# A hybrid decoder block on one core: 48 instead of 40 dense expert columns, gate2 through DRAM, and buffers laid out anew

## The chip, the cores and the metric

The kernel runs on one core of one Trainium2 chip. The metric is the device time of one execution in microseconds. The kernel before took 2249.88 us, the median of three runs (2248.31 to 2253.04).

## What is computed

One layer works on 256 tokens of width 2048 (D), in float32. A condition vector goes through one matrix, `w_ada`, and gives six vectors of length D, of which the last, gate2, scales the second sub-layer. The first sub-layer mixes tokens (gated linear recurrences and a state-space scan). The second, which the change is about, is a mixture of 16384 experts with one neuron each:

```python
# reference, cut
mod = silu(c) @ w_ada + b_ada                       # shift1, scale1, gate1, shift2, scale2, gate2
x  = x + gate1 * mix(norm(x))
h2 = rms_norm(x, norm2_g) * (1 + scale2) + shift2
# 8 heads; each takes its 16 best of 128 x 128 experts by two lists of 128 keys
expert, gate = topk_softmax(h2 @ w_q, sub_keys)     # 256 tokens x 128 experts
act = gelu(einsum(h2, u_tab[expert]))               # u_tab, v_tab: 16384 x 2048 float32
out = rms_norm(x + gate2 * einsum(gate * act, v_tab[expert]), final_norm_g)
```

`u_tab` and `v_tab` are 134 MB each. Counted from the reference's inputs, the 256 tokens choose 32768 experts; written as 128 columns of 128 experts (an expert's column is its index modulo 128), 23,659 of the choices lie in columns 0 to 87 and 21,400 in columns 0 to 79.

## The kernel before

The program is written out by hand, and each engine runs its instructions in the written order. Weights arrive in tiles `raw` of 128x1024 (512 KB), four of them at a time, loaded by SyncE's queue (and every second one by ScalarE's queue for the last part). ScalarE rounds each to a high part, VectorE subtracts for the low part (`issue_split`, lines 138 and 147), and TensorE multiplies high and low parts (`hl`, four buffers).

After the first sub-layer and the query projection come three stretches that concern us.

**The U stretch** (`u_quad`, line 1262). All activations of the first J1 = 88 columns are computed, four columns at a time: 22 quads of 8 steps, each step one `raw` tile of `u_t` and 12 matmuls of 512 columns. A quad's 128x2x512 result is stored to a DRAM table `ad`. Beside it runs background work with a budget (`bg_pay`, 1.0 a step): the top-16 searches on VectorE, then 32 one-hot steps (`onehot`, `g_step`) that scatter the gates of the last JD = 40 columns into a dense table `Wt`, and the gate2 section of `w_ada`: from step 26 on, one load of 128x256 a step (128 loads, four buffers, three loads ahead) and one multiply-add on VectorE (`gate2_tick`). Before the last quad but one, four steps (`g2_steps`) turn gate2 into two 128x1024 tiles with TensorE and ScalarE; before the last quad everything in the background is flushed, the buffers of that time are released, and two tiles of 128x4x2048 (`vs`) are cleared and first filled.

**The dense columns.** For each of the JD last columns, `u_slot` multiplies h2 with the column of `u_t` (two tiles, 16 matmuls of 512 and 16 of 256 columns), applies GELU and multiplies into `Wt`. Then, for each half of the output width, `v_slot` multiplies `Wt` with the column of `v_t` (one tile, 12 matmuls of 512) into four PSUM banks.

**The sparse experts** run beside the dense columns. A group of four tokens is one of 64 sparse quads: four GpSimd gathers fetch the up to 128 rows of `v_t` (8 KB each) of one token, rows of dense columns being skipped by a bounds check; four more fetch the 128 activations from `ad` (`w_gather`); `v_quad` (line 1343) multiplies the rows with the weights `Wz` in 16 matmuls of 32x512. There are buffers for two quads, so the gathers of quad q+2 wait until `v_quad(q)` has read its tiles. `tick` is called twice in each `u_slot` and once after each `v_slot`, 4*JD = 160 times, and issues a sparse quad whenever

```python
if n >= 6 and sq["n"] < 62 * (n - 3) // (4 * JD - 4):
    sparse()
```

that is after two or three ticks in turn (62 quads over 157 ticks). The last two quads follow the last tick.

`rows_load` fetches, at three places among the `v_slot`s, the two halves of x (from DRAM, 1 MB each) and the final norm's gain repeated on 128 partitions (1 MB) into the tile `H` that held h2. `merge` multiplies a PSUM bank with gate2 into a part of `H`, adds it to x, and squares the sum on ScalarE; `final` normalises and stores.

Of the kernel before, what the change touches and what calls it, by code (L numbers as in the profile page):

```python
# [19 lines left out]
D = 2048  # L20
# [3 lines left out]
JD = 40  # L24
# [9 lines left out]
NQ = 4  # L34
ETILES = [72]
# [22 lines left out]
def hybrid_kernel(ctx, tc, xT, cols, w_ada, w_in, lru_w, w_o1, w_o2, w_q, keys, u_t, v_t, fng, out):  # L58
# [11 lines left out]
    def bank(n):  # L70
        return psum.tile([128, 512], FT, name=f"b{n}")

# [566 lines left out]
    def lru_gates(b, i):  # L639
        h = 4 * b + i  # L640
        xc = LR["xc"][:, i]
        Z = {}

        def g_pe():
            w = LR["w"].pop(h)
            Z["p"] = p = bank(4 - (i + GD) % 2)
            for s in range(2):
                pe.matmul(p[:, s * 256:(s + 1) * 256], w[:, s], xc, start=True, stop=True)
            lru_w_load()

        def g_ew():
            if i == 0:
                LR.update(a=keep.tile([128, 4, 256], FT, name="X0"),
                          m=keep.tile([128, 4, 256], FT, name="X1"),
                          gx=keep.tile([128, 4, 256], FT, name="X2"))
# [60 lines left out]
    def evac(e, ps):  # L716
# [8 lines left out]
        elif e >= 48:  # L725
            after = None
            if e >= 64:
                g = e % 4
                if e < 68:
                    S["BC"] = S["BCs"][:, g % 2]  # L730
                    for n, t in enumerate(("xs", "zs")):
                        S[t] = (mix.tile([128, 4, 256], FT, name=t) if g == 3 else
                                keep.tile([128, 4, 256], FT, name=f"X{2 * (g % 2) + n}"))
# [77 lines left out]
    def x_load(i):  # L811
        x2[i] = keep.tile([128, 4, 256], FT, name=f"X{i}")
        sp.dma_start(x2[i], xT[:, 4 * i:4 * i + 4, :])
# [178 lines left out]
    g2 = [keep.tile([128, 1024], FT, name=f"X{i}") for i in range(2)]  # L992
# [151 lines left out]
    def g2_steps(q):  # L1144
        P = {}

        def g_pe():
            P[0] = b = gbank()
            for i in range(4):
                k = 4 * q + i  # L1150
                pe.matmul(b[:, i * 128:(i + 1) * 128], bc(mod[:, 5, k:k + 1], 128, 128), ident,
                          start=True, stop=True)

        def g_ew():
            act.activation(g2[q // 2][:, (q % 2) * 512:(q % 2 + 1) * 512], P[0], AF.Copy)
# [12 lines left out]
    def gate2_tick():  # L1168
        n = gt["n"]
        if n >= 128:  # L1170
            return
        q, k = divmod(n, 16)
        if n == 0:
            for _ in range(3):
                gate2_load()
        gate2_load()
        w = gt.pop(n)
        if k == 0:
            gt["a"] = s1.tile([128, 256], FT, name="adga", bufs=2)
# [4 lines left out]
        if k == 15:  # L1184
            a = gt["a"]

            def fin():
                p = gbank()
                for i in range(2):
                    pe.matmul(p[:, i:i + 1], a[:, i * 128:(i + 1) * 128], ones[:, 0:1], start=True, stop=True)  # L1190
                defer(lambda: dve.tensor_add(mod[:, 5, 2 * q:2 * q + 2], p[:, :2], col("b_ada", 80 + 2 * q, 2)))
# [29 lines left out]
    NG = 8  # L1221

    def onehot():
# [5 lines left out]
        a = s1.tile([128, NG, 128], F8, name="oha", bufs=4)  # L1229
        o = s1.tile([128, NG, 2, JD], F16, name="ohb", bufs=4)  # L1230
# [29 lines left out]
    ad = dram.tile([T, E1], FT, name="ad")  # L1260

    def u_quad(n, pay):
        ps = [bank(2 * (n % 2) + tb) for tb in range(2)]
        for kp in range(8):
# [14 lines left out]
            if it >= 26:  # L1279
                gt["slot"] = it  # L1280
                gate2_tick()
# [53 lines left out]
    def v_quad(q):  # L1335
# [4 lines left out]
        for c in range(4):  # L1340
            for g in range(4):
                x = 32 + 32 * (4 * (q % NW) + g) - m
                pe.matmul(sb[c][32 * g:32 * g + 32, :], Wz[:, x:x + 32], vs[q % 2][:, g, c * 512:(c + 1) * 512],  # L1343
# [92 lines left out]
    nm = [0]  # L1436
# [9 lines left out]
    def merge(tb, c, ps):  # L1446
        s = slice(c * 512, (c + 1) * 512)
        nm[0] += 1
        t = R["t"][:, 3, (nm[0] % 4) * 512:(nm[0] % 4 + 1) * 512]
        dve.tensor_tensor(t, ps, g2[c // 2][:, (c % 2) * 512:(c % 2 + 1) * 512], op=OP.mult)  # L1450
        a = R["t"][:, tb, s]
        dve.tensor_tensor(a, a, t, op=OP.add)
# [22 lines left out]
    for n in range(NU):  # L1475
        if n == 1:
            gbk[:] = [6, 7, 4, 5]
        if n == NU - 2:
            bg.extend(g2_steps(q) for q in range(4))
        if n == NU - 1:  # L1480
            bg_flush()
            assert gt["n"] == 128 and not pedue and len(gpend) == 0
            s1s.close()
            qp = ctx.enter_context(tc.tile_pool(name="qp", bufs=1))
            for i in range(2):
# [93 lines left out]
```

## Time and profile before

| | before |
|---|---|
| median of the timed runs | 2249.88 us |
| profiled execution | 2229.45 us |
| its span, first to last instruction | 2227.7 us |
| TensorE matmul busy | 2073.1 us, 93% of the span |
| VectorE / ScalarE / GpSimd busy | 65% / 38% / 42% |
| moved by DMA | 626.38 MB |
| granted TensorE clock, mean | 0.971 |

The profile is one execution, taken with the hardware profiler; a line number such as L1343 is a line of the kernel, and "PE b L1343 <- DMA vq" means that TensorE stood idle before an instruction of that line until a transfer into `vq` had landed. A matmul's end is modelled, so matmuls overlap in the rows, and the step from one start to the next is the better measure of what one costs. `PEld` is TensorE's loading of weights, beside the matmuls.

### The profile page before, as it was taken

How to read it: one execution, taken by the hardware profiler on the slowest of the kernel's cores; microseconds unless marked ns; L12 is line 12 of the kernel's file. 1: busy time of each engine (PE TensorE's matmuls, PEld its weight loads, DVE VectorE, ACT ScalarE, POOL GpSimd, SP SyncE). 2: the span in 40 equal slices, each digit the busy share in tenths (PEclk: the TensorE clock that was granted, in tenths of full speed). 3: DMA queues.
4: the chain of work that ended last, by engine and by line, in shares of the span. 5: the costliest groups of instructions: out<-in, count | busy, mean ns of one | idle time of the engine just before them, and what ended most of it. 6: DMA issues, size and time to landing. Idle time of an engine off the chain costs nothing.

```text
span 2227.7 us, 34204 instructions
## 1 busy us (share of the span) xinstructions
PE 2073.1 (93%) x12675; PEld 1619.3 (73%) x12675; DVE 1437.3 (65%) x2135; ACT 929.0 (42%) x1421; POOL 855.4 (38%) x730
## 2 busy tenths in 40 slices
PE   4889999999999999999999999999999999989996
PEld 3888999978999888888788888755555555445553
DVE  6987887988878868779989974433233343324333
ACT  2335565666644454444345444322222232223232
POOL 0002333222112010001224424377777776667774
PEclk6889999999999999999999999999999999999998
DMA  9956666667789854677777778699999999998996
GB/s 350 383 193 203 216 202 219 224 222 258 265 300 324 323 171 161 199 237 244 253 243 244 245 247 293 209 366 355 340 341 348 357 356 344 362 365 327 353 363 242
DMA packets 261686, 626.38 MB, mean 281 GB/s; under 512 B 36261, under 2 KB 144933, under 8 KB 237093
## 3 DMA queue, kind: packets, MB, share of 16 engines
q1 hardware_dynamic: 204672, 387.72, 51.4%
q0 software_dynamic: 45056, 194.01, 23.1%
q10 hardware_dynamic: 11792, 42.47, 5.5%
q8 instruction: 99, 1.62, 0.3%
q14 instruction: 67, 0.55, 0.1%
HBM read 682.97 MB, written 15.73 MB: 314 GB/s over the span
## 4 chain that ended last, share of the span: by engine, by line
PE 52%; DMA 23%; DVE 11%; issue 8%; ACT 2%; POOL 2%; POOLq 0%; SPq 0%; DVEq 0%; ACTq 0%
DMA vq<-in_v_t,X 19%; PE b L426 7%; PE b L1271 6%; PE b L1273 6%; PE b L1272 6%; PE b L1343 4%; PE b L428 3%; PE b L1426 3%; DVE hl L147 3%; PE b L898 3%; DVE aa L247 2%; PE b L792 2%; PE b L794 2%; PE b L793 2%; PE b L899 1%
## 5 line engine op out<-in xcount | busy, mean ns | idle before, releaser
L138 ACT ACTIVATE hl<-raw 128x1024 fp32r<-128x1024 f32 x578 | 612.1, 1061 | 1155.6 <-PE b L428 356.5
L147 DVE TENSOR_TENSOR hl<-raw,hl 128x1024 fp32r<-128x1024 f32 x578 | 745.8, 1295 | 138.7 <-ACT hl L138 137.5
L426 PE MATMUL b<-H,hl 128*128 128x512 f32 x1248 | 447.5, 402 | 3.1 <-DVE qT L432 2.8
L1311 POOL DMA_INDIRECT vq<-in_v_t,X x256 | 301.6, 1178 | 139.8 <-DMA vq<-in_v_t,X 60.9
L428 PE MATMUL b<-H,hl 128*128 128x256 f32 x1248 | 349.9, 280 | 5.2 <-DVE hl L147 5.2
L1343 PE MATMUL b<-vq,Wz 128*32 128x512 f32 x2048 | 290.5, 625 | 57.1 <-DMA vq<-in_v_t,X 49.7
L1321 POOL DMA_INDIRECT X<-ad,X x256 | 273.1, 1067 | 124.1 <-issue 72.9
L426 PEld LDWEIGHTS b<-H,hl 128*128 128x128 f32 x1248 | 234.4, 188 | 84.8 <-issue 25.7
L1271 PE MATMUL b<-hl,H 128*128 128x512 f32 x704 | 278.6, 396 | 0.0
L1273 PE MATMUL b<-hl,H 128*128 128x512 f32 x704 | 274.8, 390 | 3.0 <-DVE hl L147 2.9
L1272 PE MATMUL b<-hl,H 128*128 128x512 f32 x704 | 274.5, 390 | 0.0
L1343 PEld LDWEIGHTS b<-vq,Wz 128*32 128x32 f32 x2048 | 69.0, 113 | 240.9 <-issue 143.0
L428 PEld LDWEIGHTS b<-H,hl 128*128 128x128 f32 x1248 | 235.5, 189 | 6.8 <-DVE hl L147 6.6
L1426 PE MATMUL b<-hl,X 128*128 128x512 f32 x960 | 230.2, 396 | 4.7 <-ACT X L419 3.2
L1426 PEld LDWEIGHTS b<-hl,X 128*128 128x128 f32 x960 | 177.9, 189 | 70.1 <-issue 26.9
L1333 DVE TENSOR_TENSOR Wz<-X 128x4 f32<-128x4 f32 x64 | 10.5, 166 | 286.9 <-ACT X L1329 215.4
L794 PE MATMUL b<-H,hl 128*128 128x256 f32 x560 | 159.2, 284 | 6.2 <-DVE hl L147 6.2
L792 PE MATMUL b<-H,hl 128*128 128x256 f32 x560 | 161.4, 288 | 0.0
L793 PE MATMUL b<-H,hl 128*128 128x256 f32 x560 | 158.7, 283 | 0.0
L1273 PEld LDWEIGHTS b<-hl,H 128*128 128x128 f32 x704 | 132.6, 188 | 32.2 <-DVE hl L147 4.2
L1272 PEld LDWEIGHTS b<-hl,H 128*128 128x128 f32 x704 | 132.7, 189 | 25.9
L1271 PEld LDWEIGHTS b<-hl,H 128*128 128x128 f32 x704 | 132.5, 188 | 25.9
(312 smaller groups left out, 3083.6 us busy)
## 6 DMA issues: line engine op xcount, KB each, us to landing
raw<-in_u_t SPq DMA_DIRECT2D x216, 512.0 KB, 4.3
raw<-in_w_in SPq DMA_DIRECT2D x146, 512.0 KB, 4.8
adr<-in_w_ada SPq DMA_DIRECT2D x96, 512.0 KB, 4.9
adw<-in_w_ada SPq DMA_DIRECT2D x64, 512.0 KB, 8.4
raw<-in_w_o SPq DMA_DIRECT2D x64, 512.0 KB, 5.4
raw<-in_u_t ACTq DMA_DIRECT2D x40, 512.0 KB, 7.6
raw<-in_v_t SPq DMA_DIRECT2D x40, 512.0 KB, 8.3
raw<-in_v_t ACTq DMA_DIRECT2D x40, 512.0 KB, 8.0
```

The costliest lines, as they stand in the source:

```text
L138: act.activation(t[:, 0], r, AF.Copy)
L147: dve.tensor_sub(t[:, 1], r, t[:, 0].bitcast(FT))
L426: pe.matmul(ps, w[:, 0, c], x[:, k].rearrange("p a b -> p (a b)"), start=(k == 0), stop=False, skip_group_check=True)
L428: pe.matmul(ps[:, :256], w[:, 1, c], x[:, k, 0], start=False, stop=(k == 15), skip_group_check=True)
L792: pe.matmul(ps, wh, hT[:, k, 0, :], start=(k == 0), stop=False)
L1271: pe.matmul(o, hh, w[:, 0, :, kk], start=(k == 0), stop=False)
L1272: pe.matmul(o, hl_, w[:, 0, :, kk], start=False, stop=False)
L1273: pe.matmul(o, hh, w[:, 1, :, kk], start=False, stop=(k == 15))
L1311: pool.indirect_dma_start(x, None, vf, bass.IndirectOffsetOnAxis(ap=eV[:, t:t + 1], axis=0), bounds_check=E1 - 1, oob_is_err=False)
L1321: pool.indirect_dma_start(wA[:, 4 * q + g:4 * q + g + 1], None, adf, bass.IndirectOffsetOnAxis(ap=eW[:, t:t + 1], axis=0), bounds_check=T ...
L1343: pe.matmul(sb[c][32 * g:32 * g + 32, :], Wz[:, x:x + 32], vs[q % 2][:, g, c * 512:(c + 1) * 512], start=(m == 0), stop=(m == 31), skip_gr ...
L1426: pe.matmul(ob[tb * 2 + c], w[:, i, s], v[:, k, c * 512:(c + 1) * 512], start=(jj == 0 and (i, k) == (0, 0)), stop=(jj == JD - 1 and k == 1))
```

## The change

JD goes from 40 to 48: J1 falls from 88 to 80 columns, so that there are 20 U quads, 48 `u_slot`s, 96 `v_slot`s and 192 ticks; the 64 sparse quads skip the rows of 48 columns instead of 40. The wider dense table needs room, and that is what the rest does:

- the tiles X0 and X1 become halves of one tile X01; in the U stretch its halves hold the four buffers of the first one-hot operand and two (instead of four) buffers of the gate2 loads; the second one-hot operand has three buffers instead of four;
- the gate2 section of `w_ada` comes in 64 loads of 128x512, one at every second step from step 22, one load ahead; its sums are closed four times instead of eight;
- the four `g2_steps` go. gate2 is stored from its 128x16 tile to DRAM (`g2d`) before the last U quad and read back, repeated on 128 partitions, into the fourth part of `H` at the first `rows_load`;
- `merge` multiplies the PSUM bank in place, adds from PSUM, and lets the square go to PSUM;
- the gather buffers are eight tiles of 128x2048 instead of two of 128x4x2048, the last of them in X01.

```diff
-JD = 40
+JD = 48
@@
+NG = 8
@@
+    pair = keep.tile([128, 8, 256], FT, name="X01")
+
+    def xbuf(i):
+        return pair[:, 4 * i:4 * i + 4] if i < 2 else keep.tile([128, 4, 256], FT, name=f"X{i}")
@@
-    g2 = [keep.tile([128, 1024], FT, name=f"X{i}") for i in range(2)]
+    two = keep.tile([128, 8, 256], FT, name="two", tag="X01")
+    ohs = two[:, :4].rearrange("p a b -> p (a b)").bitcast(F8).rearrange("p (n t i) -> p n t i", n=4, t=NG)
+    ads = two[:, 4:]
@@
-    def g2_steps(q):
...
-        return g_pe, g_ew, 0.3
@@ def gate2_load():
-        if n < 128:
+        if n < 64:
             q, k = divmod(n, 16)
-            gt[n] = s1.tile([128, 256], FT, name="adg", bufs=4)
-            sp.dma_start(gt[n], w_ada[k * 128:(k + 1) * 128, 5 * D + q * 256:5 * D + (q + 1) * 256])
+            gt[n] = ads[:, 2 * (n % 2):2 * (n % 2) + 2].rearrange("p a b -> p (a b)")
+            sp.dma_start(gt[n], w_ada[k * 128:(k + 1) * 128, 5 * D + q * 512:5 * D + (q + 1) * 512])
@@ def gate2_tick():
         if n == 0:
-            for _ in range(3):
-                gate2_load()
+            gate2_load()
         gate2_load()
@@ def onehot():
-        a = s1.tile([128, NG, 128], F8, name="oha", bufs=4)
-        o = s1.tile([128, NG, 2, JD], F16, name="ohb", bufs=4)
+        a = ohs[:, n % 4]
+        o = s1.tile([128, NG, 2, JD], F16, name="ohb", bufs=3)
@@ def u_quad(n, pay):
-            if it >= 26:
+            if it >= 22 and it % 2 == 0:
@@ def v_gather(q):
-            x, t = vs[q % 2][:, g], tok(q, g)
+            x, t = vs[4 * (q % 2) + g], tok(q, g)
@@ def rows_load(n):
             R["t"] = keep.tile([128, 4, D], FT, name="H")
+            sp.dma_start(R["t"][:, 3], bass.AP(tensor=g2d.tensor, offset=g2d.offset, ap=[[0, 128], [1, D]]))
@@ def merge(tb, c, ps):
-        t = R["t"][:, 3, (nm[0] % 4) * 512:(nm[0] % 4 + 1) * 512]
-        dve.tensor_tensor(t, ps, g2[c // 2][:, (c % 2) * 512:(c % 2 + 1) * 512], op=OP.mult)
+        dve.tensor_tensor(ps, ps, R["t"][:, 3, s], op=OP.mult)
         a = R["t"][:, tb, s]
-        dve.tensor_tensor(a, a, t, op=OP.add)
+        dve.tensor_tensor(a, a, ps, op=OP.add)
@@
-            act.activation(t, a, AF.Square, accum_out=rf[:, tb, c:c + 1])
+            act.activation(ps, a, AF.Square, accum_out=rf[:, tb, c:c + 1])
@@ for n in range(NU):
-        if n == NU - 2:
-            bg.extend(g2_steps(q) for q in range(4))
         if n == NU - 1:
@@
-            for i in range(2):
-                vs[i] = qp.tile([128, 4, D], FT, name=f"vq{i}")
+            sp.dma_start(g2d.rearrange("o (k p) -> p (o k)", p=128), mod[:, 5])
+            for i in range(8):
+                vs[i] = (qp.tile([128, D], FT, name=f"vq{i}") if i < 7 else
+                         keep.tile([128, D], FT, name="vq7", tag="X01"))
                 pool.memset(vs[i], 0.0)
-                v_gather(i)
+                if i % 4 == 3:
+                    v_gather(i // 4)
```

Line numbers shift by a few: L1333 becomes L1327, L147 becomes L153, L130 becomes L136, L1166 becomes L1160.

Where instructions stand now is seen at three places. The first is VectorE's order in the dense columns. `Wz` is the write of the weights for one sparse quad, so it marks the quads; each `hl` row is the low part of one `raw` tile, of which there is one a tick. Before, from one quad over two more:

```order
L1333 TENSOR_TENSOR Wz<-X_7824 128x4
L147 TENSOR_TENSOR hl<-raw,hl 128x1024
L1397 TENSOR_TENSOR Wt<-Wt,xt 128x256
L432 TENSOR_TENSOR xt<-b_14544,xt 128x256
L147 TENSOR_TENSOR hl<-raw,hl 128x1024 x2
L1397 TENSOR_TENSOR Wt<-Wt,xt 128x256
L432 TENSOR_TENSOR xt<-b_14633,xt 128x256
L1333 TENSOR_TENSOR Wz<-X_7824 128x4
L147 TENSOR_TENSOR hl<-raw,hl 128x1024 x2
L1397 TENSOR_TENSOR Wt<-Wt,xt 128x256
L432 TENSOR_TENSOR xt<-b_14720,xt 128x256
L1333 TENSOR_TENSOR Wz<-X_7824 128x4
```

And of the change, from one quad to the next and on to the row ahead of a third:

```order
L1327 TENSOR_TENSOR Wz<-X_7811 128x4
L153 TENSOR_TENSOR hl<-raw,hl 128x1024 x2
L1391 TENSOR_TENSOR Wt<-Wt,xt 128x256
L438 TENSOR_TENSOR xt<-b_14928,xt 128x256
L153 TENSOR_TENSOR hl<-raw,hl 128x1024
L1327 TENSOR_TENSOR Wz<-X_7811 128x4
L153 TENSOR_TENSOR hl<-raw,hl 128x1024
L1391 TENSOR_TENSOR Wt<-Wt,xt 128x256
L438 TENSOR_TENSOR xt<-b_14977,xt 128x256
L153 TENSOR_TENSOR hl<-raw,hl 128x1024 x2
L1391 TENSOR_TENSOR Wt<-Wt,xt 128x256
L438 TENSOR_TENSOR xt<-b_15066,xt 128x256
```

Before, three tiles and then two lie between quads; now three and three (62 quads over 189 ticks).

The second place is SyncE's queue where the gate2 section begins, in the U stretch. `raw` is a weight tile, `adg` a gate2 load, `ad` the store of a quad's result. Before:

```order
L130 DMA raw<-in_u_t 128x4x256
L1166 DMA adg<-in_w_ada 128x256 x4
L130 DMA raw<-in_u_t 128x4x256
L1166 DMA adg<-in_w_ada 128x256
L130 DMA raw<-in_u_t 128x4x256
L1166 DMA adg<-in_w_ada 128x256
```

Of the change, where `two` is the tile in X01 whose second half holds the gate2 loads:

```order
L1160 DMA two<-in_w_ada 128x512 x2
L136 DMA raw<-in_u_t 128x4x256 x2
L1160 DMA two<-in_w_ada 128x512
L136 DMA raw<-in_u_t 128x4x256
L1283 DMA ad<-X_9271 128x2x512
L136 DMA raw<-in_u_t 128x4x256
L1160 DMA two<-in_w_ada 128x512
```

A load of twice the size now stands behind every second weight tile, with one load ahead instead of three.

The third place is the same queue at the end of the U stretch and at the start of the `v_slot`s. Before:

```order
L1289 DMA ad<-X_13215 128x2x512
L130 DMA raw<-in_u_t 128x4x256
L130 DMA raw<-in_u_t 128x1024 x40
L130 DMA raw<-in_v_t 128x1024 x4
L1442 DMA H<-x2d 128x2048
```

Of the change:

```order
L1283 DMA ad<-X_12594 128x2x512
L1475 DMA g2d<-mod 128x16x1
L136 DMA raw<-in_u_t 128x4x256
L136 DMA raw<-in_u_t 128x1024 x48
L136 DMA raw<-in_v_t 128x1024 x4
L1434 DMA H<-g2d 128x2048
L1436 DMA H<-x2d 128x2048
```

The store of gate2 is now ahead of the last U tile, and the repeated read of it ahead of the first half of x.

More of the change, by code (lines that the diff above doesn't have):

```diff
@@ L652, in g_ew @@
             if i == 0:
-                LR.update(a=keep.tile([128, 4, 256], FT, name="X0"),
-                          m=keep.tile([128, 4, 256], FT, name="X1"),
+                LR.update(a=xbuf(0),
+                          m=xbuf(1),
                           gx=keep.tile([128, 4, 256], FT, name="X2"))
@@ L732, in evac @@
                         S[t] = (mix.tile([128, 4, 256], FT, name=t) if g == 3 else
-                                keep.tile([128, 4, 256], FT, name=f"X{2 * (g % 2) + n}"))
+                                xbuf(2 * (g % 2) + n))
                 o = S["BC"][:, (e - 64) // 4]
@@ L811, in x_load @@
     def x_load(i):
-        x2[i] = keep.tile([128, 4, 256], FT, name=f"X{i}")
+        x2[i] = xbuf(i)
         sp.dma_start(x2[i], xT[:, 4 * i:4 * i + 4, :])
@@ L1142, in q_evac @@
             bg.extend(g_step(n) for n in range(32))
-    def g2_steps(q):
[L1145 to L1155, printed above, removed]
-        return g_pe, g_ew, 0.3
     gt = {"n": 0, "ld": 0}
@@ L1162, in gate2_load @@
         gt["ld"] += 1
-        if n < 128:
+        if n < 64:
             q, k = divmod(n, 16)
-            gt[n] = s1.tile([128, 256], FT, name="adg", bufs=4)
-            sp.dma_start(gt[n], w_ada[k * 128:(k + 1) * 128, 5 * D + q * 256:5 * D + (q + 1) * 256])
+            gt[n] = ads[:, 2 * (n % 2):2 * (n % 2) + 2].rearrange("p a b -> p (a b)")
+            sp.dma_start(gt[n], w_ada[k * 128:(k + 1) * 128, 5 * D + q * 512:5 * D + (q + 1) * 512])
     def gate2_tick():
         n = gt["n"]
-        if n >= 128:
+        if n >= 64:
             return
@@ L1178, in gate2_tick @@
         if k == 0:
-            gt["a"] = s1.tile([128, 256], FT, name="adga", bufs=2)
+            gt["a"] = (pr.tile([128, 512], FT, name="adgx", tag="xt") if q % 2 else
+                       s1.tile([128, 512], FT, name="adga"))
             dve.tensor_scalar(gt["a"], w, cact[:, 0:1], None, op0=OP.mult)
@@ L1188, in fin @@
                 p = gbank()
-                for i in range(2):
+                for i in range(4):
                     pe.matmul(p[:, i:i + 1], a[:, i * 128:(i + 1) * 128], ones[:, 0:1], start=True, stop=True)
-                defer(lambda: dve.tensor_add(mod[:, 5, 2 * q:2 * q + 2], p[:, :2], col("b_ada", 80 + 2 * q, 2)))
+                defer(lambda: dve.tensor_add(mod[:, 5, 4 * q:4 * q + 4], p[:, :4], col("b_ada", 80 + 4 * q, 4)))
             pedue.append((gt["slot"] + 2, fin))
@@ L1260, in hybrid_kernel @@
     ad = dram.tile([T, E1], FT, name="ad")
+    g2d = dram.tile([1, D], FT, name="g2d")
     def u_quad(n, pay):
@@ L1342, in v_quad @@
                 x = 32 + 32 * (4 * (q % NW) + g) - m
-                pe.matmul(sb[c][32 * g:32 * g + 32, :], Wz[:, x:x + 32], vs[q % 2][:, g, c * 512:(c + 1) * 512],
+                pe.matmul(sb[c][32 * g:32 * g + 32, :], Wz[:, x:x + 32], vs[4 * (q % 2) + g][:, c * 512:(c + 1) * 512],
                           start=(m == 0), stop=(m == 31), skip_group_check=True)
@@ L1477, in hybrid_kernel @@
             gbk[:] = [6, 7, 4, 5]
-        if n == NU - 2:
-            bg.extend(g2_steps(q) for q in range(4))
         if n == NU - 1:
             bg_flush()
-            assert gt["n"] == 128 and not pedue and len(gpend) == 0
+            assert gt["n"] == 64 and not pedue and len(gpend) == 0
             s1s.close()
             qp = ctx.enter_context(tc.tile_pool(name="qp", bufs=1))
-            for i in range(2):
-                vs[i] = qp.tile([128, 4, D], FT, name=f"vq{i}")
+            sp.dma_start(g2d.rearrange("o (k p) -> p (o k)", p=128), mod[:, 5])
+            for i in range(8):
+                vs[i] = (qp.tile([128, D], FT, name=f"vq{i}") if i < 7 else
+                         keep.tile([128, D], FT, name="vq7", tag="X01"))
                 pool.memset(vs[i], 0.0)
-                v_gather(i)
+                if i % 4 == 3:
+                    v_gather(i // 4)
         u_quad(n, 1.0)
```

3 lines of the change are left out of this document (removed).

## The prediction, made blind

> **What bounds the kernel now.** I read the page first, then busy time by stretch, then who waits for whom in the stretches that change, then single rows in order of time.
>
> ```profile
> PE 2073.1 (93%) x12675; PEld 1619.3 (73%) x12675; DVE 1437.3 (65%) x2135; ACT 929.0 (42%) x1421; POOL 855.4 (38%) x730
> ...
> DMA  9956666667789854677777778699999999998996
> GB/s 350 383 193 203 216 202 219 224 222 258 265 300 324 323 171 161 199 237 244 253 243 244 245 247 293 209 366 355 340 341 348 357 356 344 362 365 327 353 363 242
> ```
>
> TensorE is busy nearly everywhere, but from slice 27 on DMA is at nine tenths too: the last 800 us have two limits close together. The view of busy time by stretch separates the U stretch (first row), the `u_slot`s (second), the `v_slot`s (third) and the end:
>
> ```profile
> core 0: us, PE busy (x) PEld busy (x) DVE busy (x) ACT busy (x) POOL busy (x), PEclk, DMA share, GB/s
> 895.00:1409.00 514.00, 509.63 (x2726) 418.86 (x2725) 423.09 (x652) 234.77 (x304) 127.32 (x86) 1.00 0.76 246
> 1409.00:1804.00 395.00, 364.64 (x2241) 227.76 (x2239) 127.81 (x191) 114.48 (x197) 284.76 (x246) 0.99 0.91 336
> 1804.00:2200.00 396.00, 370.02 (x1984) 211.85 (x1984) 138.93 (x208) 109.68 (x192) 278.44 (x256) 0.97 0.93 348
> 2200.00:2228.00 28.00, 10.76 (x64) 2.56 (x64) 14.71 (x28) 8.51 (x19) 2.98 (x3) 0.77 0.51 188
> ```
>
> In U, TensorE is idle for 4.4 of 514 us: it alone sets the pace there. In the next 791 us it waits for the gathers; these are the PE rows of the waits, U first and the dense columns second:
>
> ```profile
> PE b L1273 <- DVE hl L147: 2.9, 2, 2.6
> ```
>
> ```profile
> PE b L1343 <- DMA vq<-in_v_t,X: 48.1, 35, 3.2
> ```
>
> The ends of matmuls are modelled, so part of the waiting hides in long bursts, and starts tell more. TensorE's rows in order of time, where a burst of L1343 is one sparse quad (x32) and a tick is 12 matmuls of L1426:
>
> ```profile
> 1429.41 3.09 PE L1343 MATMUL b<-vq,Wz 128*32 128x512 f32 x16 [3.27 <-issue]
> ...
> 1569.00 3.64 PE L1343 MATMUL b<-vq,Wz 128*32 128x512 f32 x32
> 1578.42 1.25 PE L1343 MATMUL b<-vq,Wz 128*32 128x512 f32 x6
> ...
> 1883.67 3.64 PE L1343 MATMUL b<-vq,Wz 128*32 128x512 f32 x32
> 1887.24 5.73 PE L1426 MATMUL b<-hl,X 128*128 128x512 f32 x24
> 1892.91 1.06 PE L1343 MATMUL b<-vq,Wz 128*32 128x512 f32 x6
> 1895.72 3.62 PE L1343 MATMUL b<-vq,Wz 128*32 128x512 f32 x26 [1.75 <-DMA vq<-in_v_t,X]
> 1899.27 8.49 PE L1426 MATMUL b<-hl,X 128*128 128x512 f32 x36
> 1907.69 1.06 PE L1343 MATMUL b<-vq,Wz 128*32 128x512 f32 x6
> ...
> 2193.26 3.64 PE L1343 MATMUL b<-vq,Wz 128*32 128x512 f32 x32
> ```
>
> A quad without a wait takes 3.57 us (1883.67 to 1887.24). Three v ticks take 8.42 (1899.27 to 1907.69), 2.81 each; two u ticks 5.85 (1578.42 less 1569.00 less 3.57), 2.92 each. The quad at 1892.91, after two ticks, takes 6.36, so it waits 2.79. Measured in this way over the 62 quads from the first row to the last, what exceeds 3.57 us sums to 102.3 us, and it falls almost wholly on one kind: 29 quads behind two ticks wait 90.3 us (3.1 each), 32 behind three ticks 10.3 us (0.32 each), the first 1.7.
>
> **The change part by part.** I sum against the profiled execution's 2229.45 us (span 2227.7 and 1.75 around it). It lies 20.4 us under the median of 2249.88; I carry the difference over to the median unchanged.
>
> *Two U quads fewer.* ScalarE's evacuations mark the ends of quads:
>
> ```profile
> 1322.24 1.13 ACT L1286 ACTIVATE X<-b 128x512 f32<-128x512 f32 x2
> 1343.47 1.07 ACT L1286 ACTIVATE X<-b 128x512 f32<-128x512 f32 x2
> 1365.68 1.07 ACT L1286 ACTIVATE X<-b 128x512 f32<-128x512 f32 x2
> 1390.25 1.07 ACT L1286 ACTIVATE X<-b 128x512 f32<-128x512 f32 x2
> ```
>
> By the order of the program the one-hot steps end with the 18th quad in both, so what goes are quads with nothing beside them: 1322.24 to 1365.68, **-43.4**. The quad with the `g2_steps` took 24.57 against their mean of 21.72: **-3** (their matmuls, L1151 below, are 4.2 us busy).
>
> *Wider one-hot steps, other gate2 loads.*
>
> ```profile
> L1247 PE MATMUL b<-ohb,oha 128*128 128x40 f16 x512 | 18.5, 180 | 1.0 <-POOL ohb L1236 0.7 <-POOL ohb L1235 0.3
> ...
> L1151 PE MATMUL b<-ident,mod 128*128 128x128 f32 x32 | 4.2, 274 | 0.0
> ```
>
> 512 matmuls of 40 columns become 48 wide: nothing if something other than columns sets their time, a fifth of 18.5 = 3.7 if columns do; I take the middle, **+2**. The one-hot work on VectorE and GpSimd grows by a fifth too, behind a TensorE that lacked 2.9 us of VectorE's in all of U.
>
> ```profile
> L1182 DVE SCALAR_TENSOR_TENSOR adga<-adg,cact,adga 128x256 f32<-128x256 f32 x120 | 72.8, 607 | 0.6 <-DMA adg<-in_w_ada 0.6
> ```
>
> ```profile
> L247 DVE SCALAR_TENSOR_TENSOR aa<-adw,cact,aa 128x512 f32<-128x512 f32 x112 | 76.8, 748 | 0.6 <-DMA adw<-in_w_ada 0.6
> ```
>
> On VectorE 120 of 607 ns become 60 of 748: 28 us less, worth nothing where VectorE isn't waited for. The loads have less lead: a step is 21.72/8 = 2.7 us, so two steps (5.4 us) instead of three (8.1).
>
> ```profile
> DMA to landing us min/median/max: 3.3/4.5/7.3
> ```
>
> ```profile
> raw<-in_u_t SPq DMA_DIRECT2D x216, 512.0 KB, 4.3
> ...
> X<-ad,X POOLq DMA_INDIRECT x256, 2.3
> ...
> H<-x2d SPq DMA_DIRECT2D x2, 1024.0 KB, 9.1
> ...
> H<-in_fng SPq DMA_DIRECT2D x1, 1024.0 KB, 13.8
> ```
>
> The first row is that of the gate2 loads of 128 KB; the 512 KB tiles land in 4.3. So 256 KB at about 4.5 fits into 5.4 and the slowest (7.3) is 1.9 late. Behind a late multiply-add on VectorE stand the `hl` subtractions, for which TensorE waits once its four `hl` buffers are used up. Bounds: 0, and 64 x 1.9 = 122 with every load the slowest and no cover; I take **0**, by the median.
>
> *The store of gate2*: 2048 pieces of 4 bytes. Nearest is the gather of 128 pieces of 4 bytes, 2.3 us: between 2.3 and 16 x 2.3 = 37 us. Behind it in SyncE's queue stands one U tile, then the `u_slot`s' tiles; four loaded and four split tiles are ahead of TensorE, some 8 x 2.7 = 22 us of cover, so 0 to 15; I take **+2**, near the gather. The Trainium skill (DMA: Bandwidth & Descriptors, Rules for kernel authors) speaks against this store: a last dimension that isn't contiguous is cut into one descriptor per element and should be rearranged. With the 10.5 ns a packet of its Bandwidth section the store would take an estimated 21.5 us, which would add up to 20 to my sum if nothing hid it; no row before shows it.
>
> *The dense columns.* Without any waiting, TensorE needs before 80 x 2.92 + 80 x 2.81 + 62 x 3.57 = 679.7 us; 791 less this and less 102.3 of waits leaves 9 for the rest. Of the change: 96 x 2.92 + 96 x 2.81 + 62 x 3.57 = 771.4. What of the waits stays? All quads now stand behind three ticks, the kind that waited 0.32 us: 62 x 0.32 = 19.8. Bytes allow it: 395 us at 336 and 396 at 348 GB/s are 270.5 MB; 2259 rows of 8 KB fewer are gathered (-18.5 MB), 32 tiles of 512 KB come (+16.8), and 1.05 MB of gate2, so 269.8. GpSimd issues as many gathers as before, and the granted clock was 0.97 to 0.99 here. The repeated read of gate2 is 1.05 MB at 342 GB/s, 3 us, if it moves like the rest; the repeated read of the gain took 13.8 us to land against 9.1 for as many bytes of x, so up to 5 more; I take **3**. A bank now comes free after the add, not after the multiply:
>
> ```profile
> L1452 DVE TENSOR_TENSOR H<-H 128x512 f32<-128x512 f32 x4 | 2.8, 692 | 0.1
> L1450 DVE TENSOR_TENSOR H<-b,X 128x512 f32<-128x512 f32 x4 | 2.7, 686 | 6.6 <-PE b L1343 6.6
> ```
>
> Reading PSUM (L1450) costs no more than SBUF (L1452); an add of 0.7 us for each of four banks is 0 to 2.8 where the halves change, **+1**. Writing PSUM isn't shown; the two rows being alike, I price it as SBUF, 0 with under 1 us either way. Sum: 771.4 + 19.8 + 9 + 3 + 1 = 804.2 against 791: **+13**. The 28 us of the end have the same two quads and stores.
>
> Together: -43.4 - 3 + 2 + 2 + 13 = **-29**, to 2200 in the profiled execution and **2220** as a median.
>
> **The rivals.**
>
> *DMA has room, and no quad waits.* The share of 0.91 to 0.93 isn't full, and slice 2 moved 383 GB/s. Against it: even three-tick quads waited 0.32. The dense columns then take 771.4 + 9 + 1 = 781, -10; total -52, **2198**. The Trainium skill (HBM Reference, Specifications) sides with this rival: a core that streams alone can reach about 425 GB/s, well above what I saw here.
>
> *The waits come back in part.* Three-tick quads waited little because the two-tick quad before each had waited and let the gathers run ahead; now nothing does. At 0.7 us each: 771.4 + 43.4 + 13 = 828, +37, total -6, **2244**.
>
> *The gathers keep their latency: slower.* If a quad waits as long on average whatever the distance (102.3/62 = 1.65 us), the 92 us of new matmuls are paid in full: 771.4 + 102.3 + 13 = 887, +96, total +53, **2303**. It decides from 0.79 us a quad, where the 42 us gained in U are used up. Against it: 0.32 behind three ticks, and equal bytes.
>
> *Late gate2 loads*: if a quarter are 1.9 us late and nothing hides it, 16 x 1.9 = 30: total +1, **2251**. Against it: the median of 4.5.
>
> *The store of gate2 stalls the queue*: 15 instead of 2, total -16, **2234**.
>
> **How the numbers follow.** Forecast 0.54 (its own range 2206 to 2232), room on DMA 0.16, waits in part 0.13, slower 0.08, late loads 0.05, store 0.04. The range reaches from 2190, under the second, to 2246, over the third, and leaves out the slow rival and most of the late loads. A measurement can tell 0.2%, 4.5 us. Faster: 0.54 + 0.16 + 0.08 of the third + 0.04 = 0.82; within: 0.03 + 0.04 = 0.07; slower: 0.02 + 0.08 + 0.01 = 0.11.
>
> **What would show it.** The U stretch should be 467 to 474 us, its last evacuations 21 to 23 us apart, with a few us of waits for `hl`; more waits, or waits of L1182's successor for its loads, mean late loads. The 62 quads should start about 12.2 us apart and exceed 3.57 us by 20 us in sum: under 5 means the first rival, over 49 the slow one. Rows of `raw` behind the store should land as before. The forecast is wrong if the dense columns take under 785 or over 820 us.

## The result, and the profile after

| | before | change |
|---|---|---|
| median of the timed runs | 2249.64 us (4 runs, 2248.31 to 2253.04) | 2214.41 us (4 runs, 2210.67 to 2220.39) |
| profiled execution | 2229.45 us | 2215.8 us |
| span | 2227.7 us | 2213.8 us |

The ratio of the runs is 0.9844 [0.9818, 0.9869]: 35.2 us by the medians, where 29 were forecast. The two profiled executions are only 13.7 us apart, and this difference between the medians and the profiles is the first thing to explain. Here and below, medians and ratios leave out runs that took over 1.5% longer than the fastest of their kernel.

Busy time by stretch of the change: the U stretch, the `u_slot`s, the `v_slot`s, the end (columns as in the prediction: engines' busy time, granted clock, DMA share, GB/s):

```profile
895.00:1370.00 475.00, 465.42 (x2504) 381.02 (x2503) 399.84 (x568) 217.19 (x280) 153.25 (x92) 0.99 0.74 244
1370.00:1770.00 400.00, 391.29 (x2489) 266.92 (x2489) 150.31 (x217) 133.11 (x221) 288.88 (x245) 0.99 0.90 328
1770.00:2185.00 415.00, 395.82 (x2186) 250.01 (x2184) 165.01 (x242) 134.18 (x230) 278.69 (x256) 0.98 0.92 337
2185.00:2213.80 28.80, 10.38 (x64) 2.96 (x64) 16.41 (x30) 8.69 (x19) 3.97 (x4) 0.77 0.48 176
```

U takes 475 us instead of 514, the dense columns 815 instead of 791, the end as long as before. The PE rows of the waits, over the dense columns:

```profile
PE b L1420 <- ACT X L425: 15.9, 6, 7.1
PE b L432 <- DVE xt L438: 4.9, 1, 4.9
...
PE b L1337 <- DMA vq<-in_v_t,X: 1.0, 1, 1.0
```

The 48.1 us of waiting for gathered rows (`vq`) are down to 1.0. What stays is fewer but longer waits, behind ScalarE's rounding of the dense gates `Wt` (L425; L419 before) and behind the evacuation of a `u_slot` (L438). By the starts, as in the prediction, the 62 sparse quads exceed 3.57 us by 9.9 us in sum (102.3 before).

Below I split the dense columns (first `u_slot` to last `v_slot`) of each profile with the prediction's own numbers. *Need* is 2.92 us a u tick, 2.81 a v tick, 3.57 a quad; *quads* is what the 62 quads exceed 3.57 by in sum; *rest* is what then remains. The forecast had 771.4 + 19.8 + 13 for the change; it came out as 771.4 + 9.9 + 33.

### The profile page after: what moved, and what is told of

Its sections match the earlier page's. It is cut to its first block, busy times and chain, and to the rows that moved or that the text cites. A ratio compares the mean times of both kernels' runs of the same rounds, so it can differ in the third digit from the quotient of the medians.

```text
span 2213.8 us, 34609 instructions
## 1 busy us (share of the span) xinstructions
PE 2079.3 (94%) x12899; PEld 1657.6 (75%) x12899; DVE 1463.6 (66%) x2115; ACT 955.5 (43%) x1461; POOL 887.3 (40%) x736
## 3 DMA queue, kind: packets, MB, share of 16 engines
q0 software_dynamic: 45056, 175.52, 21.4%
## 4 chain that ended last, share of the span: by engine, by line
PE 57%; DVE 15%; DMA 12%; issue 10%; POOL 4%; ACT 2%; SPq 0%; another core or an unknown queue 0%; POOLq 0%; DVEq 0%; ACTq 0%
PE b L1420 12%; PE b L1337 7%; PE b L432 6%; DMA vq<-in_v_t,X 5%; DVE hl L153 5%; PE b L1265 4%; PE b L1267 4%; PE b L1266 4%; PE b L434 3%; PE b L904 3%; DVE aa L253 3%; POOL X L1315 2%; PE b L798 2%; DMA two<-in_w_ada 2%; PE b L800 2%
## 5 line engine op out<-in xcount | busy, mean ns | idle before, releaser
L153 DVE TENSOR_TENSOR hl<-raw,hl 128x1024 fp32r<-128x1024 f32 x594 | 765.0, 1297 | 118.0 <-ACT hl L144 99.2
L432 PE MATMUL b<-H,hl 128*128 128x512 f32 x1376 | 497.2, 404 | 8.6 <-DVE xt L438 4.9
L434 PE MATMUL b<-H,hl 128*128 128x256 f32 x1376 | 387.8, 282 | 6.1 <-DVE hl L153 5.0
L432 PEld LDWEIGHTS b<-H,hl 128*128 128x128 f32 x1376 | 260.5, 189 | 97.2 <-issue 29.8
L1420 PE MATMUL b<-hl,X 128*128 128x512 f32 x1152 | 279.7, 400 | 18.7 <-ACT X L425 15.9
L1420 PEld LDWEIGHTS b<-hl,X 128*128 128x128 f32 x1152 | 216.6, 191 | 94.7 <-issue 26.4
L434 PEld LDWEIGHTS b<-H,hl 128*128 128x128 f32 x1376 | 261.8, 190 | 8.3 <-DVE hl L153 6.5
L1265 PE MATMUL b<-hl,H 128*128 128x512 f32 x640 | 254.2, 397 | 5.1 <-ACT hl L144 5.1
L1337 PE MATMUL b<-vq,Wz 128*32 128x512 f32 x2048 | 244.1, 601 | 9.2 <-DVE b L1442 6.8
L1267 PE MATMUL b<-hl,H 128*128 128x512 f32 x640 | 250.7, 392 | 2.1 <-DVE hl L153 2.1
L1266 PE MATMUL b<-hl,H 128*128 128x512 f32 x640 | 250.8, 392 | 0.0
L800 PE MATMUL b<-H,hl 128*128 128x256 f32 x560 | 159.8, 285 | 6.6 <-DVE hl L153 6.6
L798 PE MATMUL b<-H,hl 128*128 128x256 f32 x560 | 162.0, 289 | 0.0
L799 PE MATMUL b<-H,hl 128*128 128x256 f32 x560 | 159.3, 284 | 0.0
L1327 DVE TENSOR_TENSOR Wz<-X 128x4 f32<-128x4 f32 x64 | 10.6, 168 | 216.4 <-issue 71.5
L372 DVE SCALAR_TENSOR_TENSOR adacc<-adr,cact,adacc 128x1024 f32<-128x1024 f32 x90 | 128.6, 1429 | 29.0 <-DMA adr<-in_w_ada 28.8
L1265 PEld LDWEIGHTS b<-hl,H 128*128 128x128 f32 x640 | 121.0, 189 | 29.5 <-ACT hl L144 5.5
L1267 PEld LDWEIGHTS b<-hl,H 128*128 128x128 f32 x640 | 120.9, 189 | 29.1 <-DVE hl L153 3.7
```

The costliest lines, as they stand in the source:

```text
L153: dve.tensor_sub(t[:, 1], r, t[:, 0].bitcast(FT))
L432: pe.matmul(ps, w[:, 0, c], x[:, k].rearrange("p a b -> p (a b)"), start=(k == 0), stop=False, skip_group_check=True)
L434: pe.matmul(ps[:, :256], w[:, 1, c], x[:, k, 0], start=False, stop=(k == 15), skip_group_check=True)
L798: pe.matmul(ps, wh, hT[:, k, 0, :], start=(k == 0), stop=False)
L1265: pe.matmul(o, hh, w[:, 0, :, kk], start=(k == 0), stop=False)
L1266: pe.matmul(o, hl_, w[:, 0, :, kk], start=False, stop=False)
```

## The experiments

Ratios are to the kernel before, run in turn on the same chip. Its median differs between the groups of runs, so times are compared within a group and ratios across.

### Was the profiled execution of before a usual one?

The kernel before, unchanged, profiled once more.

> The kernel before, unchanged, profiled once more. Theory: the profile of before was an unusually quick execution of its dense columns (2229 us beside timed runs of 2248 to 2253), because there TensorE waits for gathers and so for whatever rate the transfers reach; this profile then has a span near 2240 to 2250 us, with dense columns of 800 to 815 us instead of 791 and a sum of waits of the 62 sparse quads of 110 to 125 us instead of 102, and the same U stretch of 514 us. Rival: the profile is typical and the timed runs carry some 20 us outside the dense columns; the span is then again 2225 to 2231 us with dense columns of 790 to 793.

It took 2253.07 us. The PE rows of its waits in the dense columns, and the row of that stretch:

```profile
PE b L1343 <- DMA vq<-in_v_t,X: 27.8, 18, 3.0
PE b L426 <- DVE Wz L1333: 13.4, 2, 11.3
PE b L1426 <- ACT X L419: 11.4, 4, 5.9
PE b L1426 <- issue: 10.7, 5, 5.4
```

```profile
1408.00:2222.00 814.00, 737.69 (x4224) 447.99 (x4223) 264.85 (x396) 223.38 (x386) 556.29 (x501) 0.96 0.91 332
```

The dense columns took 815 us, not 791; U (512.6) and the end (28.7) are as in the first profile. The 23.6 us between the two spans lie there alone. It is not the quads that are slower (73.4 us in sum, against 102.3): the rest went from 9 to 62 us, and the granted clock is 0.96 where it was 0.99 and 0.97. So the theory has the stretch right and its reason wrong: it expected 110 to 125 us at the quads. The first profile was a quick execution of just this stretch. The timed runs of before beside the first two groups of experiments (21 and 19) reach from 2228.15 to 2267.32 us, so its 2229 stands at the fast end. The second profile is no middle either: the 21 runs of its own group end at 2251.71, with a median of 2237.99.

### Which edit carries the gain?

All edits, with the 40 columns of before:

```diff
-JD = 48
+JD = 40
```

> All of the change but the number of dense columns (40, as before). Theory: the gain comes from the columns, and the other edits cost what the profile of the change shows at the end of the U stretch (about 10 us in the last quad) less 3 us for the dropped gate2 steps, and 0 to 5 us for the repeated read: 2250 to 2262 us. Rival: the layout (loads of gate2 halved in number, eight gather tiles, products in place) brings a good part of the gain: 2215 to 2240 us.

2244.0 us (12 runs, 2237.36 to 2259.64), ratio 1.0019 [0.9995, 1.0043]. The theory's 2250 to 2262 was set against a before of 2250; as a ratio it is 1.000 to 1.005, and the run falls into that. So `g2d`, the loads of 256 KB, the merge in place and the eight gather tiles together are worth nothing to 0.4%; the gain is that of the eight columns, with the spacing that they bring. Half-way:

```diff
-JD = 48
+JD = 44
```

> The change with 44 dense columns: 21 U quads, quads of sparse rows behind two or three ticks. Theory (dense columns cost the same at 40, 44 and 48 as long as the bytes are the same; only the U quads count): dense columns 805 to 818, U 493, ratio to before 0.991 to 0.995, with quads' waits between those of 40 columns (73 us) and of 48 (10). Rival (the columns' gain hangs on all quads standing behind three ticks): quads' waits back to 70, dense columns and time as at 40 columns and above, ratio 0.998 or more.

2245.9 us (10 runs), ratio 0.996 [0.9928, 0.9992]: less than half of the gain of 48, though the interval reaches into that of the theory. U took 488.9, but the dense columns 834, more than with 40 or 48, at a clock of 0.97. Equal bytes did not give equal time, so the theory is weaker than its ratio. With a fifth tile for weights:

```diff
+            if "x" in st and (n - st["x"]) % 5 == 0:
+                raws[n] = st["pool"].tile([128, 1024], FT, name="rawx")
+            else:
+                raws[n] = wp.tile([128, 1024], FT, name="raw", bufs=NRAW)
@@ before the last U quad
+            st.update(x=st["dma"], pool=qp)
+            issue_dma()
```

> As with 44 columns, with a fifth tile for weights from the last U quad on. Theory (mean rate of transfers sets the pace): within 0.2% of 44 columns with four tiles; waits move from the weight tiles to the gathers. Rival (bursts of gathers make single weight tiles late, and four tiles are too short a cover): ScalarE's waits for weight tiles fall by half or more and the time by 10 to 25 us, ratio 0.982 to 0.989.

2235.42 us (6 runs, 2220.89 to 2248.73), ratio 0.9905 [0.9861, 0.9948], between the two theories and overlapping the interval of four tiles: inconclusive.

### The change once more

> The change, timed again beside the next three kernels. Theory (transfers set the dense columns, so a stretch of as many bytes takes as long): ratio 0.982 to 0.988 as before, U near 474 us, dense columns 805 to 825, and the waits again not at the sparse quads (under 25 us in sum) but at work that ScalarE does behind a late weight tile. Rival (this profile was an unlucky one and the dense columns cost as forecast): dense columns 795 to 808, quads' waits near 20.

2219.1 us (6 runs), ratio 0.9836 [0.98, 0.9872]. The first row is its U stretch, the second its dense columns:

```profile
895.60:1373.00 477.40, 467.06 (x2504) 381.50 (x2503) 398.50 (x568) 217.34 (x280) 152.41 (x92) 0.99 0.74 242
1373.00:2192.00 819.00, 789.39 (x4674) 513.63 (x4672) 315.66 (x460) 267.42 (x450) 573.64 (x501) 0.99 0.91 332
```

U 477, dense columns 819, quads 12.9: the first profile of the change was a usual one, that of before was not.

### The store of gate2, and the last U quad

ScalarE's evacuations of the change, the last two quads of U:

```profile
1342.27 1.07 ACT L1280 ACTIVATE X<-b 128x512 f32<-128x512 f32 x2
...
1374.48 1.07 ACT L1280 ACTIVATE X<-b 128x512 f32<-128x512 f32 x2
```

32.2 us, where a quad takes 21.7. ScalarE's waits in between:

```profile
ACT hl L144 <- DMA raw<-in_u_t: 17.1, 4, 8.4
```

Here weight tiles do land late: 17.1 us, a single one 8.4. Before them in SyncE's queue stands the store of gate2, and beside them run the first gathers. To part the two, gate2 is transposed on TensorE and stored as 16 rows of 512 bytes:

```diff
-            sp.dma_start(g2d.rearrange("o (k p) -> p (o k)", p=128), mod[:, 5])
+            pe.transpose(g2p[:16, :128], mod[:, 5], ident)
...
+                act.activation(g2r, g2p[:16, :128], AF.Copy)
+                defer(lambda: sp.dma_start(g2d.rearrange("o (k p) -> (o k) p", p=128), g2r))
```

> The change, with gate2 transposed on TensorE and stored as 16 rows of 512 bytes instead of 2048 pieces of 4 bytes. Theory: the store of pieces is what holds up the U tiles behind it; the last U quad, 32.2 us in the profile of the change, comes back to 21 to 24 us, and the time falls by 8 to 11 us to 2203 to 2207 us. Rival: the first eight gathers, which start at the same place, take the transfers from the U tiles; the last quad stays at 30 us or more and the time stays at 2211 to 2218 us.

```profile
1346.45 1.07 ACT L1280 ACTIVATE X<-b 128x512 f32<-128x512 f32 x2
1373.89 1.07 ACT L1280 ACTIVATE X<-b 128x512 f32<-128x512 f32 x2
```

```profile
ACT hl L144 <- DMA raw<-in_u_t: 10.7, 5, 5.1
```

The last quad takes 27.4, U 472.1, and the waits for landings fall to 10.7 us. By time it can't be told from the change: 2208.09 us (6 runs), ratio 0.9847 [0.9818, 0.9875]. Some 5 us of the quad's excess go with this edit, the other 6 stay: neither the theory's 21 to 24 us nor the rival's 30. The edit also puts the store 10 us later (issued at 1353.8 us instead of 1343.8, behind the transposition), so the pieces and the place are not told apart. For the rest, the run with half the gathered rows (next section) helps: there the last quad takes 28.6 us, so the first gathers have some part in it.

### Do transfers set the dense columns?

By the prediction the waits of the quads are those of gathers that share a nearly full DMA. If so, fewer bytes must shorten the stretch. In the change, and then in before, the bounds check of the row gathers is halved, so that the rows of the upper half of the sparse columns are not fetched; matmuls and issues stay.

```diff
-                                    bounds_check=E1 - 1, oob_is_err=False)
+                                    bounds_check=E1 // 2 - 1, oob_is_err=False)
```

> The bounds check of the row gathers is halved, so that the rows of columns 40 to 79 are not fetched (the weights and every matmul stay; the output is not the reference's): about 10,700 rows of 8 KB, 88 of 270 MB, go from the dense columns. Theory (transfers set the dense columns): they fall from 815 to TensorE's own need of 767 plus at most 12, that is 770 to 780, the time by 35 to 45 us (ratio to before 0.965 to 0.972), and ScalarE no longer waits for weight tiles that then hold up TensorE. Rival (the 38 us come from the order of ScalarE's and VectorE's work, whatever the transfers do): dense columns stay over 805.

> The kernel before with the halved bounds check: the rows of columns 44 to 87 are not fetched (the output is not the reference's). Theory (before, transfers held the dense columns some 100 us above TensorE's need, and the change fills that gap with matmuls): dense columns fall from 790 to 815 us to 700 to 720, the waits of the quads to under 25, ratio 0.950 to 0.965; the fall is four to five times that of the same edit in the change (17 to 20 us). Rival (the quads wait for the latency of a gather or for its issue on GpSimd, whatever its bytes): dense columns stay over 770, ratio over 0.98.

The gathers' queue in the page (packets, MB, share) of before, and of before with half the rows:

```profile
q0 software_dynamic: 45056, 194.01, 23.1%
```

```profile
q0 software_dynamic: 45056, 96.86, 13.7%
```

The dense columns of the change with half the rows, and of before with half the rows:

```profile
1366.00:2164.00 798.00, 787.05 (x4673) 511.05 (x4672) 316.28 (x462) 267.20 (x450) 568.74 (x502) 1.00 0.73 236
```

```profile
1409.00:2240.00 831.00, 741.70 (x4222) 452.88 (x4221) 264.51 (x396) 223.29 (x386) 548.92 (x501) 0.94 0.66 213
```

In the change this gives 2191.96 us, ratio 0.9711 [0.9667, 0.9755]: 27 us less than the change beside it, 17 to 21 of them in the dense columns. The ratio lies in the theory's range, the dense columns (798 against 770 to 780) do not. In **before** it gives nothing: 2247.9 us (6 runs, 2247.06 to 2273.62; two more took 2290), ratio 1.0006 [0.9968, 1.0043]. Against the second profile of before the DMA share falls from 0.91 to 0.66 and the quads' waits from 73 to 39 us, and the stretch is 17 us longer (this execution, at 2267, took 19 us more than the median). What the quads no longer wait reappears as rest (113 us), at a granted clock of 0.94. The theory that transfers held these columns some 100 us above TensorE's need, mine here and the prediction's by its reading of a nearly full DMA, falls. The rival's figures came (over 770, ratio over 0.98), but not its mechanism as it stood: the quads' waits did shrink.

### Does TensorE set them?

The opposite test: the kernel before with 43.8 us more of matmuls in its `u_slot`s, without new tiles or transfers.

```diff
+            for kk in range(3 if after and not h else 0):
+                wide(p, w, kk, h2, kk)
             for kk in range(8):
                 wide(p, w, kk, h2, 8 * h + kk)
```

> The kernel before, in which each of the 40 u_slots first does 3 of its 16 pairs of matmuls once more, into the bank that the real ones then start afresh: 40 x 3 x 0.365 = 43.8 us more of TensorE's work in the first half of the dense columns, about what the eight new u_slots of the change add there (46.7), with no new tile, no new transfer and the ticks where they were. Theory (with 40 columns TensorE has slack in the dense columns, whatever holds it up, and added matmuls fall into it; this and the two U quads are the whole change): dense columns 790 to 830 as in the looks at before, ratio 0.997 to 1.007. Rival (matmuls are paid for in full, and the change's columns were cheap for another reason, the even spacing of the sparse quads behind three ticks): dense columns 835 to 875, ratio 1.014 to 1.022.

```profile
1409.00:2210.00 801.00, 757.87 (x4457) 476.06 (x4456) 264.60 (x395) 223.00 (x385) 555.90 (x501) 0.99 0.92 337
```

2244.33 us (12 runs), ratio 1.0016 [0.999, 1.0043]: 43.8 us of TensorE's work for next to nothing (by the interval, under 10 us). The dense columns took 802, between the two profiles of before; the quads' waits fell to 43 us and the rest to 35. With 40 columns TensorE has slack here that added work takes up.

### Does it matter where the quads stand?

The change, its sparse quads behind two and four ticks in turn instead of three:

```diff
-        if n >= 6 and sq["n"] < 62 * (n - 3) // (4 * JD - 4):
+        if sq["n"] < 62 and n >= 7 + 3 * sq["n"] - sq["n"] % 2:
```

> The change, with the sparse quads behind two and four ticks in turn instead of three and three; the same work. Theory: waits for gathers come from uneven distance (3.1 us behind two ticks, 0.3 behind three), so the 31 quads behind two ticks wait 60 to 95 us in sum again and the time is 2265 to 2300 us. Rival: only the work per quad counts (12.2 us of TensorE against some 11.4 of transfers), the wait after two ticks is small: under 15 us in sum, and the time stays at 2210 to 2225 us.

```profile
1374.00:2250.00 876.00, 799.62 (x4674) 518.47 (x4672) 317.01 (x463) 267.22 (x452) 553.10 (x504) 0.97 0.87 312
```

```profile
PE b L1420 <- ACT X L425: 43.2, 17, 5.4
PE b L432 <- DVE xt L438: 12.5, 7, 5.5
```

2266.3 us (6 runs, 2249.73 to 2274.05; two more took 2283.78 and 2313.82), ratio 1.0104 [1.007, 1.0137]: the same work and bytes, some 60 us more. The quads themselves wait 8.6 us only, against the theory's 60 to 95: its time came by another way. The loss is in the ticks, behind ScalarE's rounding of `Wt` and the evacuations. So slack is not all: the gain of the change needs the even spacing too.

### More weight tiles for fewer gather tiles

```diff
-            x, t = vs[4 * (q % 2) + g], tok(q, g)
+            x, t = vs[i % 7], tok(*divmod(i, 4))
@@
+            if "x" in st and (n - st["x"]) % 6 < 2:
+                raws[n] = st["two"][:, (n - st["x"]) % 6]
```

> The change with seven gather tiles instead of eight; the eighth becomes two more tiles for weights, so six in all, from the last U quad on. Theory (with 48 columns the 17 to 20 us above the run with half the rows are single weight tiles that bursts of gathers make late; the gathers have slack): dense columns fall to 797 to 806, the quads' waits stay under 25, ratio to before 0.975 to 0.981. Rival (the mean rate of transfers sets them): dense columns within 4 us of 814 to 819 with the waits moved to the quads (30 and more), ratio 0.983 or above.

2233.17 us (6 runs), ratio 0.9917 [0.9898, 0.9935].

```profile
PE b L1338 <- DMA vq<-in_v_t,X: 12.5, 7, 3.8
PE b L1338 <- issue: 4.8, 8, 1.1
```

The rest falls from 33 to 11 us, but the quads' waits rise from 10 to 47: with seven tiles of lead instead of eight the gathers are late again, and the dense columns take 830. The rival has the waits and the ratio right, but not the length (within 4 us of 814 to 819). As the edit takes a gather tile and adds two weight tiles at once, it doesn't show what six weight tiles are worth alone. The store as rows on top of this:

> Six weight tiles and seven gather tiles, and gate2 stored as 16 rows of 512 bytes. Theory (the two gains add): U 470 to 473, its last quad 25 to 28 us instead of 32, dense columns 797 to 806, ratio 0.973 to 0.979. Rival (the store's cost is hidden once six weight tiles are there): within 0.2% of six weight tiles alone.

2224.8 us (4 runs), ratio 0.988 [0.9859, 0.99]; U 470.9 against 480.6. By the medians the store is worth 8 us here, though the two intervals touch; both the theory's ratio and the rival's were missed. Neither of the two beats the change.

## Why the prediction was right, and where it wasn't

| dense columns, us | length | need | quads | rest | clock |
|---|---|---|---|---|---|
| before, the profile of the prediction | 791 | 680 | 102 | 9 | 0.98 |
| before, second profile | 815 | 680 | 73 | 62 | 0.96 |
| before, half the rows | 832 | 680 | 39 | 113 | 0.94 |
| before, 43.8 us of matmuls more | 802 | 724 | 43 | 35 | 0.99 |
| the change's layout, 40 columns | 808 | 680 | 73 | 55 | 0.97 |
| 44 columns | 834 | 726 | 31 | 77 | 0.97 |
| 44 columns, five weight tiles | 822 | 726 | 25 | 71 | 0.96 |
| the change | 815 | 771 | 10 | 33 | 0.98 |
| the change, second profile | 819 | 771 | 13 | 35 | 0.99 |
| the change, store as rows | 813 | 771 | 24 | 17 | 1.00 |
| the change, half the rows | 798 | 771 | 17 | 10 | 1.00 |
| the change, six weight tiles | 830 | 771 | 47 | 11 | 0.99 |
| the change, six weight tiles, store as rows | 826 | 771 | 46 | 9 | 0.99 |
| the change, quads behind 2 and 4 ticks | 876 | 771 | 9 | 96 | 0.97 |

Each entry is rounded by itself. The sum of quads and rest is steadier than its parts: the three profiles of the change that differ at most in the store have 43, 48 and 41 us in sum, divided 10 and 33, 13 and 35, 24 and 17.

The time came within the range and near the number, 5.6 us under it. Step by step:

- **Two U quads fewer, -43.4 with -3 and +2.** Right in kind, 3 to 7 us too large: U lost 39.3 us between the first profiles, 35.1 between the second ones, where 42.4 were forecast (with +2 for the one-hot steps), and its 475.0 and 477.5 us lie above the 467 to 474 that were to show the forecast right. The missing part is the last quad, 32.2 and 31.4 us, where 21 to 23 were expected. The store, **+2** with bounds of 0 and 15, is 3 to 10 of it, its later place included (U of 472.1 against 475.0 and 477.5, of 470.9 against 480.6). The Trainium skill's rule against it (DMA: Bandwidth & Descriptors, Rules for kernel authors) agrees in its sign; the estimate of 21.5 us made from that page's price was too high: in the change the pieces ran within some 7 us (1349 to 1356). The other 6 us of that quad I put down to the first gathers; half the rows took back some 3 of them, the remainder is argued, not shown.
- **Late gate2 loads, 0.** Right for the time, but the loads were late, the sign that the prediction had set for this rival. VectorE waited for them about 30 us in sum in U of the change; these are the two largest entries (us, times):

```profile
DVE adgx L1176: 17.3, 12
DVE adga L1176: 8.0, 7
```

It stayed hidden: these are TensorE's waits for the split tiles in that stretch, of which the first lies in the last quad, when all gate2 loads were done, and only the second (2.1 us) can stand behind a late load.

```profile
PE b L1265 <- ACT hl L144: 5.1, 1, 5.1
PE b L1267 <- DVE hl L153: 2.1, 2, 1.1
```

- **Dense columns, +13 to 804.** 815 and 819: within the bounds set (785 to 820). The quads' 19.8 were 9.9 and 12.9, and 23.8 with the store as rows; the claim that all of them would now be of the quick kind holds. What failed is the **9 for the rest**: 33 and 35. The +3 for the repeated read and the +1 for the merge show in no run by themselves; with this layout and 40 columns the stretch took 808, between the two profiles of before.
- **The end, 0.** 28.3 before, 29.3 and 27.6 after.
- **"I carry the difference over to the median unchanged."** This step failed most. The 20.4 us were not something beside the sum but an unusually good rest in the very stretch I was pricing. Against the second profile of before the dense columns change by next to nothing (815 against 815 and 819), not by +13. That profile is at the slow end of its group; if what parts each first group's median from its profile lies in this stretch alone, the medians 2249.64 and 2214.41 stand for 811 and 813 us of dense columns. So the median gains about what U gains, 35 to 39 us. Two errors, a U gain some 5 us too large and dense columns some 11 too long, cancel in part and leave the 6 us; that much of the hit is luck.
- **The reason for the quads' waits.** Transfers near their limit: wrong for before. Halving the gathered bytes there freed no time, and neither that nor 43.8 us of added matmuls moved the stretch out of 791 to 832 us. Of the rivals, the one in which DMA has room (2198) has its premise from this test, but not its time: what the quads don't wait goes to the rest. The rate by which the Trainium skill sided with it (HBM Reference, Specifications: some 425 GB/s for one core alone) was reached in no run here: the dense columns moved 312 to 342 GB/s, and with half the rows 213 to 236.

What the change does, then, as far as shown: it puts 92 us of matmuls into a stretch whose length with 40 columns was set neither by the gathered bytes nor by TensorE's matmuls alone, spaces its quads evenly, and so saves two U quads at little cost there. After it, TensorE's need fills 94% of the stretch, transfers begin to count (17 to 21 us), and waits that go from one place turn up at another.

**What stays open** is what sets the 800 us with 40 columns. One thing can be said of the rest: as far as the records go it is not late weight tiles, my theory halfway. In the dense columns of the change ScalarE's splits stood idle for 518 us; the semaphore records show TensorE's increment at the end of 355 of them, a tile's landing at the end of none, and for the remainder they have nothing. This is one of these splits, at the passage from the `u_slot`s to the `v_slot`s, with the end of the tick before it on TensorE:

```profile
1771.31 0.28 PE L434 MATMUL b<-H,hl 128*128 128x256 f32 x1
...
1775.71 1.06 ACT L144 ACTIVATE hl<-raw 128x1024 fp32r<-128x1024 f32 x1 [5.09 <-remote]
...
1778.68 1.65 PE L1420 MATMUL b<-hl,X 128*128 128x512 f32 x3 [7.10 <-ACT X L425]
```

The wait's releaser is not named. By the trace's packets the tile's last one landed at 1766.27; by its semaphore records TensorE's increment, for matmuls that the rows end by 1771.59, came at 1775.66. ScalarE had waited for TensorE, whose increment came 4 us later than its modelled ends say, and then TensorE waited 7.10 us for ScalarE. In the quick profile of before no such increment of the dense columns came over 1.5 us late; in its second profile 56 of 440 recorded ones did (the quick one has 521 records there, so some are missing), with half the rows 70 of 425, in the change 48 of 457. What makes them late was not isolated. The granted clock is lowest in the same runs, but a halved clock can be the effect of a stall as well as its cause, and no run here kept it up. It is not the whole of it: at half clock stood 31 us of these columns in the quick profile, 65 in the second, 92 with half the rows, and at most half of such time is lost, where the rests are 9, 62 and 113.

A rival that no run tests is the issue of the gathers on GpSimd. These are two of its waits in the dense columns of before with half the rows:

```profile
POOL vq L1311 <- PE b L1343: 114.2, 23, 10.8
POOL X L1321 <- issue: 72.5, 238, 0.3
```

Some 0.3 us stand before each gather. In the profile of the prediction its 501 gathers of this stretch are 563 us busy, with these pauses some 714: more than TensorE's 680 with 40 columns, less than the 771 with 48. That would give TensorE slack whatever the bytes, and every run here kept the number of gathers. Against GpSimd as the only cause stands the first row: it waits for `v_quad` too. (Over the whole span it is 38% busy and ScalarE 42%; the table of the profile before has the two exchanged.)

## What to carry to other kernels

Profile the kernel before twice before summing against one profile: here two executions differed by 24 us in the very stretch that the change touches, while the three timed runs on record lay within 5 us of each other. A stretch where an engine is 90% busy can still take up added work for next to nothing, and a wait that names a transfer doesn't prove that bytes are the limit; adding work to one resource and taking bytes from the other told this here in two runs. Where in-order engines pass work in a ring, keep the background work evenly spaced: here unequal gaps cost some 60 us with the same work.

## What the runs showed of the hardware

TensorE's halved clock appears in spells, and its cost is in the rows. After a stall in the change:

```profile
1444.55 0.77 PE L432 MATMUL b<-H,hl 128*128 128x512 f32 x1 [4.88 <-DVE xt L438]
1445.11 0.42 PE L434 MATMUL b<-H,hl 128*128 128x256 f32 x1
1445.33 0.63 PE L432 MATMUL b<-H,hl 128*128 128x512 f32 x1
1445.76 0.41 PE L434 MATMUL b<-H,hl 128*128 128x256 f32 x1
1445.97 0.63 PE L432 MATMUL b<-H,hl 128*128 128x512 f32 x1
```

A pair takes 0.64 us (1445.33 to 1445.97) instead of 0.365 (2.92/8); the trace has the granted clock at 0.50 from 1442.6 to 1449.4. The Trainium skill (TensorE: Matmul & The Clock Gate, The HAM clock gate) has the clock halved after an idle window of about 3.4 us; the 4.88 us of idling ahead of these rows agree. So a long wait is paid for again in the matmuls behind it, and the sum of a kernel's waits understates it.

A gathered row that the bounds check leaves out is still a packet: 45056 on the gathers' queue with all rows and with half of them. And with a store of 8 KB in pieces of 4 bytes U took 3 to 10 us longer than with as many bytes in 16 rows, issued 10 us later.
